# Row-wise cosine similarity: another order of rows for the loads, one square moved between engines, and the last load split

## Chip, cores, metric

The kernel runs on one core of one Trainium2 chip. Four of the core's engines occur here: ACT (ScalarE) and DVE (VectorE) compute, POOL (GpSimd) issues the loads, SP (SyncE) issues the store. The 16 DMA engines move the data in packets. The metric is the device time of one execution in microseconds, the median over several executions. A comparison is made between executions of two kernels on the same chip.

## The reference

```python
x = np.random.randn(8192, 8192).astype(np.float32)
y = np.random.randn(8192, 8192).astype(np.float32)

def reference(x, y):
    x_norm = np.linalg.norm(x, axis=1, keepdims=True)
    y_norm = np.linalg.norm(y, axis=1, keepdims=True)
    return np.sum(x * y, axis=1) / (x_norm.squeeze() * y_norm.squeeze() + 1e-8)
```

Two matrices of 268 MB each are read once. The output has 8192 numbers.

## The kernel before

Rows are spread over the 128 partitions (P = 128) as 64 tiles (T = 64) of 128 rows. Partition `p` of tile `t` holds row `64 p + t`, so within one load the rows of neighbouring partitions lie 64 rows, 2 MiB, apart. That distance is called the pitch here. The loads are issued from POOL and convert fp32 to fp16 on the way.

```python
    C1 = 5462 if C == 8192 else (2 * C) // 3
    x_re = x.rearrange("(p t) c -> t p c", t=T)
    y_re = y.rearrange("(p t) c -> t p c", t=T)
    out_re = out.rearrange("(p t) -> p t", t=T)
    data = ctx.enter_context(tc.tile_pool(name="data", bufs=2))
    # ... scratch and statistics tiles cut ...
    for t in range(T):
        x_tile = data.tile([P, C], fp16)
        y_tile = data.tile([P, C], fp16)
        nc.gpsimd.dma_start(out=x_tile, in_=x_re[t])
        nc.gpsimd.dma_start(out=y_tile, in_=y_re[t])
        # ACT: sum of x*x over the whole row; sum of y*y over the first C1 columns
        nc.scalar.activation(out=act_scr, in_=x_tile, func=Square, accum_out=nx2[:, t : t + 1])
        nc.scalar.activation(out=act_scr[:, :C1], in_=y_tile[:, :C1], func=Square,
                             accum_out=ny2a[:, t : t + 1])
        # DVE: sum of x*y over the whole row; sum of y*y over the other columns
        nc.vector.tensor_tensor_reduce(out=dve_scr, in0=x_tile, in1=y_tile, ...,
                                       accum_out=dot[:, t : t + 1])
        nc.vector.tensor_tensor_reduce(out=dve_scr[:, C1:], in0=y_tile[:, C1:],
                                       in1=y_tile[:, C1:], ..., accum_out=ny2b[:, t : t + 1])
    # ny2 = ny2a + ny2b; res = dot / (sqrt(nx2 * ny2) + 1e-8), all 128x64   (cut)
    nc.sync.dma_start(out=out_re, in_=res)
```

(`Square` stands for the long enum name; arguments are shortened.)

Of the kernel before, what the change touches and what calls it, by code (L numbers as in the profile page):

```python
# [1 line left out]

# [4 lines left out]


@with_exitstack
def kernel(  # L10
    ctx: ExitStack,
    tc: tile.TileContext,
    x: bass.AP,
    y: bass.AP,
    out: bass.AP,
):
    nc = tc.nc
    P = nc.NUM_PARTITIONS
    R, C = x.shape
    assert R % P == 0  # L20
    T = R // P

    fp32 = mybir.dt.float32
    fp16 = mybir.dt.float16

    C1 = 5462 if C == 8192 else (2 * C) // 3

    x_re = x.rearrange("(p t) c -> t p c", t=T)
    y_re = y.rearrange("(p t) c -> t p c", t=T)
    out_re = out.rearrange("(p t) -> p t", t=T)  # L30

    data = ctx.enter_context(tc.tile_pool(name="data", bufs=2))
    scratch = ctx.enter_context(tc.tile_pool(name="scratch", bufs=1))
    stats = ctx.enter_context(tc.tile_pool(name="stats", bufs=1))

    dve_scr = scratch.tile([P, C], fp16)
    act_scr = scratch.tile([P, C], fp16)

    nx2 = stats.tile([P, T], fp32)
    ny2a = stats.tile([P, T], fp32)  # L40
    ny2b = stats.tile([P, T], fp32)
    dot = stats.tile([P, T], fp32)
    res = stats.tile([P, T], fp32)

    for t in range(T):
        x_tile = data.tile([P, C], fp16)
        y_tile = data.tile([P, C], fp16)
        nc.gpsimd.dma_start(out=x_tile, in_=x_re[t])  # L48
        nc.gpsimd.dma_start(out=y_tile, in_=y_re[t])  # L49

        nc.scalar.activation(  # L51
            out=act_scr,
            in_=x_tile,
            func=mybir.ActivationFunctionType.Square,
            accum_out=nx2[:, t : t + 1],
        )
        nc.scalar.activation(  # L57
            out=act_scr[:, :C1],
            in_=y_tile[:, :C1],
            func=mybir.ActivationFunctionType.Square,  # L60
            accum_out=ny2a[:, t : t + 1],
        )
        nc.vector.tensor_tensor_reduce(  # L63
            out=dve_scr,
            in0=x_tile,
            in1=y_tile,
            scale=1.0,
            scalar=0.0,
            op0=mybir.AluOpType.mult,
            op1=mybir.AluOpType.add,  # L70
            accum_out=dot[:, t : t + 1],
        )
        nc.vector.tensor_tensor_reduce(  # L73
            out=dve_scr[:, C1:],
            in0=y_tile[:, C1:],
            in1=y_tile[:, C1:],
            scale=1.0,
            scalar=0.0,
            op0=mybir.AluOpType.mult,
            op1=mybir.AluOpType.add,  # L80
            accum_out=ny2b[:, t : t + 1],
        )

    ny2 = stats.tile([P, T], fp32)
    nc.vector.tensor_add(out=ny2, in0=ny2a, in1=ny2b)  # L85
    prod = stats.tile([P, T], fp32)
    nc.vector.tensor_mul(out=prod, in0=nx2, in1=ny2)  # L87
    denom = stats.tile([P, T], fp32)
    nc.scalar.activation(  # L89
        out=denom,  # L90
        in_=prod,
        func=mybir.ActivationFunctionType.Sqrt,
        bias=0.0,
        scale=1.0,
    )
    nc.vector.tensor_single_scalar(  # L96
        out=denom, in_=denom, scalar=1e-8, op=mybir.AluOpType.add
    )
    rden = stats.tile([P, T], fp32)
    nc.vector.reciprocal(out=rden, in_=denom)  # L100
    nc.vector.tensor_mul(out=res, in0=dot, in1=rden)  # L101

    nc.sync.dma_start(out=out_re, in_=res)


# [1 line left out]
_INS = ['x', 'y']  # L107
_OUTS = [((8192,), 'float32')]


# [23 lines left out]
```

## Time and profile before

| | before |
|---|---|
| median time | 1267.15 us |
| span of the profiled execution | 1265.6 us |
| first y tile ready for ACT | 25.5 us |
| last y tile ready for ACT | 1249.4 us |
| store of the result issued | 1263.2 us |

The page of the kernel before. "DMA" is the mean busy share of the 16 DMA engines in tenths, in 40 equal slices of the span. "GB/s" is what they wrote in each slice; the source bytes are twice that, because fp32 becomes fp16. The last line is the head of the chain of waits.

```profile
span 1265.6 us, 1011 instructions
DVE 751.0 (59%) x261; ACT 768.9 (61%) x259; POOL 67.9 (5%) x132
...
DMA  9999999999999999999999999999999999999994
GB/s 182 214 213 212 217 216 216 215 216 217 217 217 216 216 216 215 216 216 216 217 216 216 216 216 214 216 217 217 217 216 217 215 216 216 216 216 217 216 217 93
...
q0 software_dynamic: 18432, 268.44, 99.8%
...
DMA 96%; DVE 3%; issue 1%; POOL 0%; ACT 0%; DVEq 0%; POOLq 0%; PEldq 0%
```

The DMA engines never rest, and DVE and ACT do for 40% of the time. The kernel is bound by its loads. Stretches chosen by hand (columns: stretch in us, its length, busy time of DVE, ACT and POOL with instructions, clock, DMA share, GB/s written):

```profile
0.00:40.00 40.00, 11.71 (x4) 17.30 (x6) 3.51 (x10) 1.00 0.95 189
40.00:120.00 80.00, 46.85 (x16) 48.83 (x17) 4.22 (x8) 1.00 1.01 212
120.00:200.00 80.00, 46.85 (x16) 50.01 (x18) 4.22 (x8) 1.00 1.02 216
```

Part of the low first line is the start, before the first load runs.

Two lines from the start of the timeline of the kernel before, and its end (start, length, engine, line, operation, output<-inputs, and what ended the idle time before it). In the loop ACT waits for each load, so the starts of its squares tell when a load is ready. The first two lines are the second load, which is the first of y, and the eleventh:

```profile
25.47 4.75 ACT L57 ACTIVATE act_scr<-y_tile 128x5462 f16<-128x5462 f16 x1 [3.41 <-DMA y_tile<-in_y_dram]
...
115.01 7.03 ACT L51 ACTIVATE act_scr<-x_tile 128x8192 f16<-128x8192 f16 x1 [5.20 <-DMA x_tile<-in_x_dram]
...
1230.07 4.75 ACT L57 ACTIVATE act_scr<-y_tile 128x5462 f16<-128x5462 f16 x1 [2.51 <-DMA y_tile<-in_y_dram]
...
1249.44 4.75 ACT L57 ACTIVATE act_scr<-y_tile 128x5462 f16<-128x5462 f16 x1 [2.56 <-DMA y_tile<-in_y_dram]
1249.52 8.69 DVE L63 CUSTOM_DVE_ANT_0 dve_scr<-x_tile,y_tile 128x8192 f16<-128x8192 f16 x1 [7.63 <-DMA y_tile<-in_y_dram]
...
1258.25 3.00 DVE L73 CUSTOM_DVE_ANT_0 dve_scr<-y_tile 128x2730 f16<-128x2730 f16 x1
...
1262.99 0.23 DVE L101 TENSOR_TENSOR res<-dot,rden 128x64 f32<-128x64 f32 x1
1263.24 0.37 SPq L103 DMA_DIRECT2D out_dram<-res  x1
```

A y tile is ready every 19.37 us. After the last one nothing is left to load, and DVE's 8.69 and 3.00 us lie bare, then 2 us of small operations, then the store until 1265.6.

### The profile page before, as it was taken

The page shows a single profiled execution, that of the slowest core. Times are in us where ns is not written, and L with a number is a line of the kernel's source. Part 1 is how long each engine was busy: PE and PEld are TensorE (multiplying, and loading weights), DVE is VectorE, ACT ScalarE, POOL GpSimd, SP SyncE. Part 2 cuts the span into 40 slices and gives each one's busy share as a digit, 9 for nine tenths or more (in the row PEclk, how much of TensorE's full clock was granted, in tenths as well). Part 3 has the DMA queues.
Part 4 walks back from the last instruction along what each step waited for, and adds up shares of the span by engine and source line. Part 5 has one row for each costly group of instructions (what it writes and reads, how often), then busy time and mean ns, then how long its engine had stood idle before and what let it go on. Part 6 is the DMA issues. An engine that isn't in the chain of part 4 may idle for free.

```text
span 1265.6 us, 1011 instructions
## 1 busy us (share of the span) xinstructions
DVE 751.0 (59%) x261; ACT 768.9 (61%) x259; POOL 67.9 (5%) x132
## 2 busy tenths in 40 slices
DVE  1565655755656657557566565575565665755756
ACT  4656666666566566665665666656656656666564
POOL 0000000000000000000000000000000000000000
DMA  9999999999999999999999999999999999999994
GB/s 182 214 213 212 217 216 216 215 216 217 217 217 216 216 216 215 216 216 216 217 216 216 216 216 214 216 217 217 217 216 217 215 216 216 216 216 217 216 217 93
DMA packets 18584, 268.54 MB, mean 212 GB/s; under 512 B 2192, under 2 KB 2192, under 8 KB 2192
## 3 DMA queue, kind: packets, MB, share of 16 engines
q0 software_dynamic: 18432, 268.44, 99.8%
q14 instruction: 8, 0.07, 0.0%
q1 hardware_dynamic: 144, 0.03, 0.0%
HBM read 536.87 MB, written 0.03 MB: 424 GB/s over the span
## 4 chain that ended last, share of the span: by engine, by line
DMA 96%; DVE 3%; issue 1%; POOL 0%; ACT 0%; DVEq 0%; POOLq 0%; PEldq 0%
DMA y_tile<-in_y_dram 96%; DVE dve_scr L63 3%; DVE dve_scr L73 0%; POOL x_tile L48 0%; DVE rden L100 0%; POOL y_tile L49 0%; ACT denom L89 0%; DVE ny L85 0%; DVE prod L87 0%; DVE res L101 0%; DVE denom L96 0%; DVEq L63 0%; DVE dot L63 0%; DVEq L85 0%; POOLq L129 0%
## 5 line engine op out<-in xcount | busy, mean ns | idle before, releaser
L63 DVE CUSTOM_DVE_ANT_0 dve_scr<-x_tile,y_tile 128x8192 f16<-128x8192 f16 x64 | 556.3, 8693 | 509.5 <-DMA y_tile<-in_y_dram 509.5
L51 ACT ACTIVATE act_scr<-x_tile 128x8192 f16<-128x8192 f16 x64 | 449.9, 7030 | 321.9 <-DMA x_tile<-in_x_dram 321.9
L57 ACT ACTIVATE act_scr<-y_tile 128x5462 f16<-128x5462 f16 x64 | 304.3, 4755 | 164.3 <-DMA y_tile<-in_y_dram 164.3
L73 DVE CUSTOM_DVE_ANT_0 dve_scr<-y_tile 128x2730 f16<-128x2730 f16 x64 | 192.2, 3003 | 2.2
L48 POOL DMA_DIRECT2D x_tile<-in_x_dram x64 | 33.9, 530 | 996.8 <-DVE dot L63 996.0
L49 POOL DMA_DIRECT2D y_tile<-in_y_dram x64 | 33.8, 528 | 158.7 <-DVE ny2b L73 146.0
L57 ACT ACTIVATION_READ_ACCUMULATOR act_scr<-y_tile 128x1 f32 x64 | 11.9, 186 | 0.0
L51 ACT ACTIVATION_READ_ACCUMULATOR act_scr<-x_tile 128x1 f32 x64 | 11.9, 186 | 0.0
L73 DVE DVE_READ_ACCUMULATOR2_ANT ny2b<- 128x1 f32 x64 | 5.3, 83 | 0.0
L63 DVE DVE_READ_ACCUMULATOR2_ANT dot<- 128x1 f32 x64 | 5.3, 83 | 0.0
L89 ACT ACTIVATE denom<-prod 128x64 f32<-128x64 f32 x1 | 0.3, 256 | 6.3 <-DVE prod L87 6.3
L51 ACT ACT_TABLE_LOAD x1 | 1.3, 1283 | 0.7 <-PEq L118 0.7
L89 ACT ACT_TABLE_LOAD x1 | 1.3, 1283 | 0.0
L100 DVE RECIPROCAL rden<-denom 128x64 f32<-128x64 f32 x1 | 0.6, 553 | 0.0
L96 DVE TENSOR_SCALAR denom<-denom 128x64 f32<-128x64 f32 x1 | 0.2, 195 | 0.3 <-ACT denom L89 0.3
L85 DVE TENSOR_TENSOR ny<-ny2a,ny2b 128x64 f32<-128x64 f32 x1 | 0.2, 225 | 0.1
L101 DVE TENSOR_TENSOR res<-dot,rden 128x64 f32<-128x64 f32 x1 | 0.2, 226 | 0.0
L87 DVE TENSOR_TENSOR prod<-nx,ny 128x64 f32<-128x64 f32 x1 | 0.2, 224 | 0.0
L118 POOL MEMSET const-float32-0.0<- 128x1 f32 x1 | 0.1, 98 | 0.2 <-issue 0.2
L118 POOL MEMSET const-bfloat16-1.0<- 128x1 bf16 x1 | 0.1, 102 | 0.0
L118 POOL MEMSET const-float32-1.0<- 128x1 f32 x1 | 0.1, 98 | 0.0
L118 POOL MEMSET const-uint8-127<- 128x1 uint8 x1 | 0.1, 98 | 0.0
## 6 DMA issues: line engine op xcount, KB each, us to landing
x_tile<-in_x_dram POOLq DMA_DIRECT2D x64, 2048.0 KB, 19.7
y_tile<-in_y_dram POOLq DMA_DIRECT2D x64, 2048.0 KB, 26.3
out_dram<-res SPq DMA_DIRECT2D x1, 32.0 KB, 1.5
```

Source lines behind the costliest of these rows:

```text
L48: nc.gpsimd.dma_start(out=x_tile, in_=x_re[t])
L49: nc.gpsimd.dma_start(out=y_tile, in_=y_re[t])
L51: nc.scalar.activation(out=act_scr, in_=x_tile, func=mybir.ActivationFunctionType.Square, accum_out=nx2[:, t : t + 1],)
L57: nc.scalar.activation(out=act_scr[:, :C1], in_=y_tile[:, :C1], func=mybir.ActivationFunctionType.Square, accum_out=ny2a[:, t : t + 1],)
L63: nc.vector.tensor_tensor_reduce(out=dve_scr, in0=x_tile, in1=y_tile, scale=1.0, scalar=0.0, op0=mybir.AluOpType.mult, op1=mybir.AluOpType ...
L73: nc.vector.tensor_tensor_reduce(out=dve_scr[:, C1:], in0=y_tile[:, C1:], in1=y_tile[:, C1:], scale=1.0, scalar=0.0, op0=mybir.AluOpType.mult,
L85: nc.vector.tensor_add(out=ny2, in0=ny2a, in1=ny2b)
L87: nc.vector.tensor_mul(out=prod, in0=nx2, in1=ny2)
L89: nc.scalar.activation(out=denom, in_=prod, func=mybir.ActivationFunctionType.Sqrt, bias=0.0, scale=1.0,)
L96: nc.vector.tensor_single_scalar(out=denom, in_=denom, scalar=1e-8, op=mybir.AluOpType.add)
L100: nc.vector.reciprocal(out=rden, in_=denom)
L118: nc = _bacc.Bacc("TRN2", target_bir_lowering=False, num_devices=1)
```

## The change

There are three intents. The rows are grouped in blocks of 8, so that the pitch falls to 8 rows (256 KiB) and one load reads within 32 MiB instead of 256. The whole square of y goes to ACT. The last pair of tiles is loaded and worked through in pieces, so that less work is left after the last landing. The output is then stored in runs of 8 numbers (32 bytes) instead of 64.

```diff
-    C1 = 5462 if C == 8192 else (2 * C) // 3
-    x_re = x.rearrange("(p t) c -> t p c", t=T)      # y alike
-    out_re = out.rearrange("(p t) -> p t", t=T)
+    B = 8
+    x_re = x.rearrange("(a p b) c -> a b p c", p=P, b=B)      # y alike
+    out_re = out.rearrange("(a p b) -> p a b", p=P, b=B)
 ...
-    for t in range(T):
+    for t in range(T - 1):
-        nc.gpsimd.dma_start(out=x_tile, in_=x_re[t])
+        nc.gpsimd.dma_start(out=x_tile, in_=x_re[t // B, t % B])
 ...
         nc.scalar.activation(
-            out=act_scr[:, :C1], in_=y_tile[:, :C1],
+            out=act_scr, in_=y_tile,
 ...
-        nc.vector.tensor_tensor_reduce(     # DVE's part of y*y
-            out=dve_scr[:, C1:], in0=y_tile[:, C1:], in1=y_tile[:, C1:], ...
+    # last pair: x in 2 loads of 4096 columns, y in loads of 4096, 2048, 2048 columns;
+    # ACT squares each piece; DVE forms x*y over each piece of y
+    # five additions of 128x1 join the pieces; then prod, sqrt, + 1e-8, reciprocal, product
 ...
-    nc.sync.dma_start(out=out_re, in_=res)
+    nc.sync.dma_start(out=out_re, in_=res.rearrange("p (a b) -> p a b", b=B))
```

More of the change, by code (lines that the diff above doesn't have):

```diff
@@ L24 @@
     fp16 = mybir.dt.float16
-    C1 = 5462 if C == 8192 else (2 * C) // 3
-    x_re = x.rearrange("(p t) c -> t p c", t=T)
-    y_re = y.rearrange("(p t) c -> t p c", t=T)
-    out_re = out.rearrange("(p t) -> p t", t=T)
+    B = 8
+    x_re = x.rearrange("(a p b) c -> a b p c", p=P, b=B)
+    y_re = y.rearrange("(a p b) c -> a b p c", p=P, b=B)
+    out_re = out.rearrange("(a p b) -> p a b", p=P, b=B)
     data = ctx.enter_context(tc.tile_pool(name="data", bufs=2))
@@ L39, with finalize @@
     nx2 = stats.tile([P, T], fp32)
-    ny2a = stats.tile([P, T], fp32)
-    ny2b = stats.tile([P, T], fp32)
+    ny2 = stats.tile([P, T], fp32)
     dot = stats.tile([P, T], fp32)
     res = stats.tile([P, T], fp32)
-    for t in range(T):
+    prod = stats.tile([P, T], fp32)
+    denom = stats.tile([P, T], fp32)
+    rden = stats.tile([P, T], fp32)
+    def finalize(lo, hi):
+        s = slice(lo, hi)
+        nc.vector.tensor_mul(out=prod[:, s], in0=nx2[:, s], in1=ny2[:, s])
+        nc.scalar.activation(
+            out=denom[:, s],
+            in_=prod[:, s],
+            func=mybir.ActivationFunctionType.Sqrt,
+            bias=0.0,
+            scale=1.0,
+        )
+        nc.vector.tensor_single_scalar(
+            out=denom[:, s], in_=denom[:, s], scalar=1e-8, op=mybir.AluOpType.add
+        )
+        nc.vector.reciprocal(out=rden[:, s], in_=denom[:, s])
+        nc.vector.tensor_mul(out=res[:, s], in0=dot[:, s], in1=rden[:, s])
+    CH = C // 2
+    ycuts = [0, C // 2, (3 * C) // 4, C]
+    NYC = len(ycuts) - 1
+    nx2q = stats.tile([P, 2], fp32)
+    ny2q = stats.tile([P, NYC], fp32)
+    dotq = stats.tile([P, NYC], fp32)
+    H = T // 2
+    for t in range(T - 1):
         x_tile = data.tile([P, C], fp16)
         y_tile = data.tile([P, C], fp16)
-        nc.gpsimd.dma_start(out=x_tile, in_=x_re[t])
-        nc.gpsimd.dma_start(out=y_tile, in_=y_re[t])
+        nc.gpsimd.dma_start(out=x_tile, in_=x_re[t // B, t % B])
+        nc.gpsimd.dma_start(out=y_tile, in_=y_re[t // B, t % B])
         nc.scalar.activation(
@@ L57 @@
         nc.scalar.activation(
-            out=act_scr[:, :C1],
-            in_=y_tile[:, :C1],
+            out=act_scr,
+            in_=y_tile,
             func=mybir.ActivationFunctionType.Square,
-            accum_out=ny2a[:, t : t + 1],
+            accum_out=ny2[:, t : t + 1],
         )
@@ L72 @@
         )
+    tl = T - 1
+    x_tile = data.tile([P, C], fp16)
+    y_tile = data.tile([P, C], fp16)
+    for h in range(2):
+        cs = slice(h * CH, (h + 1) * CH)
+        nc.gpsimd.dma_start(out=x_tile[:, cs], in_=x_re[tl // B, tl % B][:, cs])
+    for j in range(NYC):
+        cs = slice(ycuts[j], ycuts[j + 1])
+        nc.gpsimd.dma_start(out=y_tile[:, cs], in_=y_re[tl // B, tl % B][:, cs])
+    for h in range(2):
+        cs = slice(h * CH, (h + 1) * CH)
+        nc.scalar.activation(
+            out=act_scr[:, cs],
+            in_=x_tile[:, cs],
+            func=mybir.ActivationFunctionType.Square,
+            accum_out=nx2q[:, h : h + 1],
+        )
+    for j in range(NYC):
+        cs = slice(ycuts[j], ycuts[j + 1])
+        nc.scalar.activation(
+            out=act_scr[:, cs],
+            in_=y_tile[:, cs],
+            func=mybir.ActivationFunctionType.Square,
+            accum_out=ny2q[:, j : j + 1],
+        )
         nc.vector.tensor_tensor_reduce(
-            out=dve_scr[:, C1:],
-            in0=y_tile[:, C1:],
-            in1=y_tile[:, C1:],
+            out=dve_scr[:, cs],
+            in0=x_tile[:, cs],
+            in1=y_tile[:, cs],
             scale=1.0,
@@ L80 @@
             op1=mybir.AluOpType.add,
-            accum_out=ny2b[:, t : t + 1],
+            accum_out=dotq[:, j : j + 1],
         )
-    ny2 = stats.tile([P, T], fp32)
-    nc.vector.tensor_add(out=ny2, in0=ny2a, in1=ny2b)
-    prod = stats.tile([P, T], fp32)
-    nc.vector.tensor_mul(out=prod, in0=nx2, in1=ny2)
-    denom = stats.tile([P, T], fp32)
-    nc.scalar.activation(
-        out=denom,
-        in_=prod,
-        func=mybir.ActivationFunctionType.Sqrt,
-        bias=0.0,
-        scale=1.0,
-    )
-    nc.vector.tensor_single_scalar(
-        out=denom, in_=denom, scalar=1e-8, op=mybir.AluOpType.add
-    )
-    rden = stats.tile([P, T], fp32)
-    nc.vector.reciprocal(out=rden, in_=denom)
-    nc.vector.tensor_mul(out=res, in0=dot, in1=rden)
-    nc.sync.dma_start(out=out_re, in_=res)
+    nc.vector.tensor_add(out=nx2[:, tl : tl + 1], in0=nx2q[:, 0:1], in1=nx2q[:, 1:2])
+    nc.vector.tensor_add(out=ny2q[:, 0:1], in0=ny2q[:, 0:1], in1=ny2q[:, 1:2])
+    nc.vector.tensor_add(out=ny2[:, tl : tl + 1], in0=ny2q[:, 0:1], in1=ny2q[:, 2:3])
+    nc.vector.tensor_add(out=dotq[:, 0:1], in0=dotq[:, 0:1], in1=dotq[:, 1:2])
+    nc.vector.tensor_add(out=dot[:, tl : tl + 1], in0=dotq[:, 0:1], in1=dotq[:, 2:3])
+    finalize(0, T)
+    nc.sync.dma_start(out=out_re, in_=res.rearrange("p (a b) -> p a b", b=B))
 _INS = ['x', 'y']
```

## The prediction

> **What bounds the kernel.** Reading. The slices show the DMA engines at 90% or more in 39 of 40 slices; the software queue holds 99.8% of 16 engines' span. DVE is 59% busy, ACT 61%. The chain of waits is 95.5% y loads; POOL waits 996 us for the dot product to free x buffers, but in time: at 1220.0 us it issues an x load, while the DMA still has 10 us of y queued ahead of it. In steady state a pair of tiles lands every 19.37 us (y landings at 1210.7, 1230.0, 1249.4): 8.39 MB of fp32 read in that time is 433 GB/s. The Trainium skill ("DMA: Bandwidth & Descriptors", Where 436 GB/s comes from) puts the fabric's limit at 435 GB/s; the trace agrees to 0.5% if the source bytes are counted. So the loop can hardly get faster.
>
> **Tail now.** The last y lands at 1249.4. Then come the dot product (8.69 us), DVE's share of the y square (3.00), about 2.0 of small operations, and the output store from 1263.2 to 1265.6 (2.4).
>
> **What the change does.**
> 1. DVE's y share (192 us in all) moves to ACT: per pair DVE falls from 11.7 to 8.8 us, ACT rises from 12.1 to about 14.4 (7.03+0.19, twice), still under 19.37. Worth nothing in 63 of 64 pairs; y loads are issued about 2.5 us sooner, into a queue that is already full.
> 2. Row layout: the pitch between partitions falls from 2 MiB to 256 KiB. The same Trainium skill page (Latency and other measured facts) reports copies losing rate at 2 MiB pitch, 164 against 214 GB/s. This trace does not show that loss: 433 GB/s is read at 2 MiB. The layout should thus give nothing, perhaps 1 to 3 us of the early slices that run at 212 to 214 GB/s instead of 217.
> 3. Split last tile. The slope between DVE's two shapes (8.69 us for 8192, 3.00 for 2730) gives 1.04 ns an element plus 0.16 us, hence 4.43, 2.29, 2.29 us for the y pieces of 4096, 2048, 2048. The first piece lands about 4.8 us before the last. DVE then works through a backlog and ends about 4.6 us after the last landing, where before it needed 11.9. ACT ends at about +2.9, its table load (1.28) at +4.2: hidden. Five additions of 128x1, estimated at 0.19 each, cost +0.95; one 128x64 addition goes (-0.25). The result is ready at about +7.2 instead of +13.86: 6.6 us saved.
> 4. Output: pieces of 32 bytes instead of 256, about 1024 data packets instead of 128, so 64 per engine instead of 8. The 256-byte packets took 18 ns each; an estimate is +1 to +2 us at the very end, all exposed.
> 5. Three more loads, smaller packets: +0.1 to 0.3 us.
>
> Sum: 1267.15 - 6.6 + 1.3 + 0.2 = about **1262 us** (-0.4%). Range 1256.5 to 1266. Chances: faster by over 2% 0.02, within 2% 0.95, slower 0.03.
>
> **What would show it.** The steady pair period stays at 19.3 to 19.5 us, mean rate 216 GB/s written; DVE busy falls by about 190 us and ACT rises by about 145 with the time hardly moving; the last DVE dot piece ends 4 to 5 us after the last y landing; the store takes 3.3 to 4.5 us from issue to the end; ACT's table load isn't on the chain.
>
> **What would make it wrong.** HBM answers differently to the 256 KiB pitch (slices well off 216 all along); the 32-byte store costs over 3 us and eats the tail's gain; the last pieces land unevenly across engines, so that the small ones come together and the backlog grows; 128x1 additions cost much more than estimated.

## More of the kernel before

The experiments ran on four chips, called chip 7, 9, 1 and 10 after the number in their records. The number of the chip of the first pair of runs isn't recorded.

## The result, and the profile after

The changed kernel takes **1255.94 us** (median of 7 executions, 1255.76 to 1256.43), the kernel before 1267.15 us. The ratio is 0.991, with a 95% interval of 0.990 to 0.992. The gain of 11.2 us is twice the predicted 5.1, and the time lies just below the range given.

From the page of the changed kernel:

```profile
span 1254.2 us, 902 instructions
DVE 558.7 (45%) x141; ACT 915.0 (73%) x265; POOL 69.5 (6%) x135
...
GB/s 198 216 214 216 217 217 218 217 216 216 216 215 217 218 217 217 217 216 216 217 216 215 217 217 217 217 217 216 216 217 214 217 217 217 217 217 217 216 216 139
```

Its stretches:

```profile
0.00:40.00 40.00, 8.70 (x2) 22.36 (x6) 3.53 (x10) 1.00 0.96 202
40.00:120.00 80.00, 34.80 (x8) 57.27 (x18) 4.25 (x8) 1.00 1.02 217
120.00:200.00 80.00, 36.80 (x9) 59.06 (x17) 4.21 (x8) 1.00 1.02 216
```

And the same two loads and the end of its timeline:

```profile
23.49 7.03 ACT L82 ACTIVATE act_scr<-y_tile 128x8192 f16<-128x8192 f16 x1 [2.59 <-DMA y_tile<-in_y_dram]
...
110.66 7.03 ACT L76 ACTIVATE act_scr<-x_tile 128x8192 f16<-128x8192 f16 x1 [2.56 <-DMA x_tile<-in_x_dram]
...
1225.17 7.03 ACT L82 ACTIVATE act_scr<-y_tile 128x8192 f16<-128x8192 f16 x1 [2.56 <-DMA y_tile<-in_y_dram]
...
1239.92 4.42 DVE L124 CUSTOM_DVE_ANT_0 dve_scr<-x_tile,y_tile 128x4096 f16<-128x4096 f16 x1 [5.97 <-issue]
...
1246.48 2.29 DVE L124 CUSTOM_DVE_ANT_0 dve_scr<-x_tile,y_tile 128x2048 f16<-128x2048 f16 x1
...
1247.39 1.28 ACT L49 ACT_TABLE_LOAD   x1
1248.69 0.09 DVE L124 DVE_READ_ACCUMULATOR2_ANT dotq<- 128x1 f32 x1
...
1250.85 0.22 DVE L60 TENSOR_TENSOR res<-dot,rden 128x64 f32<-128x64 f32 x1
1251.10 0.41 SPq L140 DMA_DIRECT2D out_dram<-res  x1
```

The y tile of the last pair but one is ready at 1225.2 instead of 1230.1, so 4.9 us were won before the tail begins. Early on, the stretch from 40 to 120 us now runs at the full rate, and the eleventh load is ready at 110.7 instead of 115.0 (starts of ACT's squares in the two timelines): 4.35 of the 4.9 us come from the first eleven loads.

The last landing isn't a wait in this timeline, because DVE and ACT are behind by then. By the completion events in the traces the last load landed at 1244.7 us, and at 1249.4 in the kernel before (the last data packets end 0.3 us earlier in both). The spans then divide like this:

| part | before | after | difference | predicted |
|---|---|---|---|---|
| until the last landing | 1249.4 | 1244.7 | -4.7 | +0.2 |
| last landing to issue of the store | 13.9 | 6.4 | -7.5 | -6.6 |
| store to the end | 2.3 | 3.1 | +0.7 | +1.3 |
| span | 1265.6 | 1254.2 | -11.4 | -5.1 |

### The profile page after: what moved, and what is told of

The parts are those of the page before. It is cut to its first block, busy times and chain, and to the rows that moved or that the text cites. A ratio compares the mean times of both kernels' runs of the same rounds, so it can differ in the third digit from the quotient of the medians. Undisturbed runs are those within 1.5% of the kernel's fastest.

```text
span 1254.2 us, 902 instructions
## 1 busy us (share of the span) xinstructions
DVE 558.7 (45%) x141; ACT 915.0 (73%) x265; POOL 69.5 (6%) x135
## 4 chain that ended last, share of the span: by engine, by line
DMA 93%; issue 5%; ACT 1%; DVE 1%; POOL 0%; POOLq 0%; DVEq 0%; PEldq 0%; ACTq 0%
DMA y_tile<-in_y_dram 93%; ACT act_scr L82 1%; DVE dve_scr L124 0%; POOL x_tile L73 0%; POOL x_tile L104 0%; DVE rden L59 0%; POOL y_tile L74 0%; ACT denom L49 0%; DVE prod L48 0%; DVE res L60 0%; DVE denom L56 0%; DVE ny L136 0%; DVE dot L138 0%; DVE dotq L124 0%; DVE dotq L137 0%
## 5 line engine op out<-in xcount | busy, mean ns | idle before, releaser
L88 DVE CUSTOM_DVE_ANT_0 dve_scr<-x_tile,y_tile 128x8192 f16<-128x8192 f16 x63 | 547.6, 8693 | 685.8 <-DMA y_tile<-in_y_dram 685.8
L76 ACT ACTIVATE act_scr<-x_tile 128x8192 f16<-128x8192 f16 x63 | 442.8, 7029 | 171.6 <-DMA x_tile<-in_x_dram 171.6
L82 ACT ACTIVATE act_scr<-y_tile 128x8192 f16<-128x8192 f16 x63 | 442.9, 7030 | 161.2 <-DMA y_tile<-in_y_dram 161.2
L124 DVE CUSTOM_DVE_ANT_0 dve_scr<-x_tile,y_tile 128x2048 f16<-128x2048 f16 (+1 forms) x3 | 8.8, 3000 | 6.0 <-issue 6.0
L118 ACT ACTIVATE act_scr<-y_tile 128x2048 f16<-128x2048 f16 (+1 forms) x3 | 7.4, 2468 | 0.2 <-DMA y_tile<-in_y_dram 0.2
L110 ACT ACTIVATE act_scr<-x_tile 128x4096 f16<-128x4096 f16 x2 | 7.2, 3608 | 0.0
L76 ACT ACT_TABLE_LOAD x1 | 1.3, 1283 | 0.7 <-PEq L155 0.7
L49 ACT ACT_TABLE_LOAD x1 | 1.3, 1283 | 0.0
```

The costliest lines, as they stand in the source:

```text
L49: nc.scalar.activation(out=denom[:, s], in_=prod[:, s], func=mybir.ActivationFunctionType.Sqrt, bias=0.0, scale=1.0,)
L76: nc.scalar.activation(out=act_scr, in_=x_tile, func=mybir.ActivationFunctionType.Square, accum_out=nx2[:, t : t + 1],)
L82: nc.scalar.activation(out=act_scr, in_=y_tile, func=mybir.ActivationFunctionType.Square, accum_out=ny2[:, t : t + 1],)
L110: nc.scalar.activation(out=act_scr[:, cs], in_=x_tile[:, cs], func=mybir.ActivationFunctionType.Square, accum_out=nx2q[:, h : h + 1],)
L118: nc.scalar.activation(out=act_scr[:, cs], in_=y_tile[:, cs], func=mybir.ActivationFunctionType.Square, accum_out=ny2q[:, j : j + 1],)
L124: nc.vector.tensor_tensor_reduce(out=dve_scr[:, cs], in0=x_tile[:, cs], in1=y_tile[:, cs], scale=1.0, scalar=0.0, op0=mybir.AluOpType.mult ...
```

## Experiments

Theory A: the first reads at a pitch of 2 MiB are slow, and the new layout takes that away. (A place, below, is the stretch of memory from which one partition reads its rows. At a pitch of 2 MiB there are 128 of x and 128 of y.) Rival B: because DVE no longer squares y, its tiles come free sooner, y loads are issued 2.5 us earlier, and a fuller queue gives the loop its gain. B is weakened already by the trace: the first four loads are issued before any tile comes free, and they are where 3.2 us of the 4.35 arise.

### e1: the row layout alone

```diff
-    x_re = x.rearrange("(p t) c -> t p c", t=T)      # y alike
-    out_re = out.rearrange("(p t) -> p t", t=T)
+    B = 8
+    x_re = x.rearrange("(a p b) c -> a b p c", p=P, b=B)      # y alike
+    out_re = out.rearrange("(a p b) -> p a b", p=P, b=B)
```

(with the indexing and the store that go with it; nothing else of the kernel before is touched)

> Only the row layout (pitch 256 KiB, output in pieces of 32 bytes) in the kernel before. Theory A (the 2 MiB pitch makes the first reads slow): the first y tile is ready near 23.5 us instead of 25.5, the eleventh load is ahead by 4.3 us, the store costs 0.75 us more: about 1263.2 us. Rival B (y loads issued earlier, because DVE no longer squares y, fill the queue): nothing gained in the loop, the store costs 0.75: about 1267.9 us.

Measured: 1263.19 us (1263.06 to 1263.69), correct. The time of theory A is met, and so are its early loads: the first y tile is ready at 23.44 us, the eleventh load at 110.60. But the kernel before took **1293.87 us** on this chip (chip 7; 1286.55 to 1302.97 in 11 executions), so the ratio is 0.976. The layout alone is worth 31 us here.

### e2: the changed kernel with the layout undone

```diff
-    x_re = x.rearrange("(a p b) c -> a b p c", p=P, b=B)      # y alike
-    out_re = out.rearrange("(a p b) -> p a b", p=P, b=B)
+    x_re = x.rearrange("(p t) c -> t p c", t=T)      # y alike
+    out_re = out.rearrange("(p t) -> p t", t=T)
```

> The changed kernel with the row layout undone (pitch 2 MiB, output in pieces of 256 bytes). Theory A: the slow first reads are back (+4.7 us), the store is 0.75 us shorter: about 1259.9 us. Rival B: the loop keeps its gain and the store gets shorter: about 1255.2 us.

Measured on chip 7: 1291.26 us (1290.23 to 1292.67), correct; ratio to before 0.997 (0.994 to 1.001). Both times expected are missed, since neither knew of this chip. The direction is A's: without the layout the loop's gain is gone. The row of GB/s by slice of this run shows where:

```profile
GB/s 173 207 210 215 216 213 213 213 214 214 210 213 213 209 208 213 208 209 214 204 212 210 211 211 207 216 214 215 214 215 209 213 215 212 214 211 213 213 210 115
```

On this chip a 2 MiB pitch is slow throughout, though not evenly (most slices lie between 204 and 216). In the packet records 2243 of its 16 KB packets took over 1.24 us, where the usual one takes 1.227; these are called slow below. The kernel before on its own chip had 318 of them, 201 in the first 120 us. In e1, on the same chip as e2, there were 21. What slow packets took beyond 1.227 us, summed and divided by the 16 DMA engines, is called their excess: 28.6 us in e2, 4.5 in the kernel before, of which 3.5 fall in the first 120 us.

### e3: the square of y on ACT, alone

```diff
-            out=act_scr[:, :C1],
-            in_=y_tile[:, :C1],
+            out=act_scr,
+            in_=y_tile,
 ...
-        nc.vector.tensor_tensor_reduce(     # DVE's part of y*y, and the addition of the parts
-            out=dve_scr[:, C1:], ...
```

> The kernel before with the whole square of y on ACT, nothing else. Theory A: only the tail gains, DVE's 3.00 us of y square and one addition of 0.25: about 1263.9 us; the first loads as slow as before (first y near 25.5 us, ACT starting on it). Rival B: 4 to 5 us more are gained in the loop: about 1259.2 us.

Measured on chip 7: 1292.76 us (1287.87 to 1297.43), correct; ratio 0.999 (0.995 to 1.003). Inconclusive in size, as 3 us drown in this chip's scatter. No sign of a gain in the loop, against B. It was run again as e11.

### e4: the pitch switched in the middle

```diff
-        nc.gpsimd.dma_start(out=x_tile, in_=x_re[t])
+        nc.gpsimd.dma_start(out=x_tile, in_=x_lo[t // 8, t % 8] if t < 32 else x_re[t])      # y alike
```

`x_lo` is the layout with blocks of 8 rows, over rows 0 to 4095. The result is wrong.

> Wrong result on purpose: in the kernel before, tiles 0 to 31 read rows 0 to 4095 at a pitch of 256 KiB, tiles 32 to 63 read as before at 2 MiB, so that half of the 2 MiB regions are read for the first time near 625 us. Theory A1 (a first read of many far apart places at once is slow): the first loads are as fast as in the changed kernel (-4.4 us by the eleventh load), and 1 to 4.4 us are lost again within some six loads after 625 us: 1264 to 1267 us. Theory A2 (a 2 MiB pitch is slow only at the start, while the DMA engines run in step): nothing is lost near 625 us, about 1262.8 us.

Measured on chip 7: 1281.38 us (1278.74 to 1284.56). Both times are missed, for the chip is slow at 2 MiB in any case. The first half had one slow packet after the first load, and the others began at the switch (623.5 us). To tell more, a chip was wanted on which the slow packets end by themselves. That came with e13.

### e5: as far apart, but no power of two

```diff
-        nc.gpsimd.dma_start(out=x_tile, in_=x_re[t])      # row 64 p + t
+        nc.gpsimd.dma_start(out=x_tile, in_=x_63[t])      # row 63 p + t; y alike
```

The result is wrong: partition p reads row 63 p + t.

> Wrong result on purpose: the kernel before, with partition p of tile t reading row 63 p + t instead of 64 p + t, so that the pitch is 2 MiB less 32 KiB: as far apart as before, but no power of two. Theory P (the power of two makes the reads collide): no slow packets, neither early (first y ready near 23.5 us) nor later, about 1262.4 us on any chip (the layout-only run less 0.75 us for its store). Theory F (first reads of many far apart places are slow): the early loads are as slow as in the kernel before (first y ready at 25.4 us or later), and 3 to 5 us of the loss stay. On a chip on which the kernel before takes 1294 us the two may share the loss: P takes away the slow packets from 200 us on, F keeps those of the first 120 us.

Measured on chip 9, where the kernel before takes 1267.27 us: 1262.65 us (1262.52 to 1262.68); ratio 0.996 (0.995 to 0.997). The first y tile is ready at 23.6 us, 20 packets are slow instead of hundreds, and the rate from 40 to 120 us is 216 GB/s (columns as above):

```profile
40.00:120.00 80.00, 46.84 (x16) 48.32 (x18) 4.22 (x8) 1.00 1.01 216
```

Theory F, in the form that a first read of far apart places is slow whatever the pitch, falls. The power of two matters, as theory P has it: places nearly as far apart, at a pitch of 2016 KiB, are read at the full rate from the start. (This is one other pitch; no more were tried.)

### e6 and e9: short reads ahead of the loads

```diff
+    first = scratch.tile([P, 2, 4, 64], fp16)
+    for k, src in enumerate((x, y)):
+        nc.gpsimd.dma_start(
+            out=first[:, k],
+            in_=src.rearrange("(p t) c -> p t c", t=T)[:, 0:4, 0:64],
+        )
     for t in range(T):
```

In e6 this stands in the kernel before. In e9 it stands in the kernel of e5, with t=63 in place of T.

> The kernel before, with two short loads ahead of all others that read 256 bytes of the rows that tiles 0 to 3 begin with, from each of the 128 places of x and of y. They delay the first load by 1 to 3 us. Theory F: the slow part moves into these short loads, which wait for all places at once; the four following loads then take 9.7 us each, and by the eleventh load the kernel is 1 to 3 us ahead of the kernel before. Theory P: the loads behind them are as slow as before, and the whole is 1 to 3 us behind the kernel before.

> Wrong result on purpose: the run with a pitch of 63 rows plus the same two short loads ahead, from its own 128 places of x and of y. If the short loads took their 10 us (first load ready at 25.3 us instead of 14.9) because the places lie a power of two apart, they take clearly less here: first load ready near 16 to 19 us, total about 1265 to 1268 us. If short casting loads take that long anyway, the first load is ready near 24 to 25 us again and the total is about 1273 us; then the run with the short loads ahead says less about the places.

Measured: e6 1274.93 us (1274.25 to 1275.54) on chip 9, correct, 7.7 us over the kernel before there (ratio 1.006). e9 1264.16 us (1264.10 to 1264.78) on chip 1, only 1.5 us over e5's 1262.65, and 0.8 below the range expected; its first load is ready at 15.3 us, also a little earlier than expected. The issue lines of the two traces (output<-source, queue, operation, count, KB written, us from issue to landing), e6 first:

```profile
first<-in_x_dram POOLq DMA_DIRECT2D x1, 64.0 KB, 8.7
first<-in_y_dram POOLq DMA_DIRECT2D x1, 64.0 KB, 13.1
```

```profile
first<-in_x_dram POOLq DMA_DIRECT2D x1, 64.0 KB, 2.7
first<-in_y_dram POOLq DMA_DIRECT2D x1, 64.0 KB, 3.0
```

The same number of equally short reads takes 3.2 and 4.4 times as long when the rows lie 2 MiB apart. So short reads that convert aren't slow by themselves. And after them, in e6, the large loads at 2 MiB pitch run at nearly the full pace: ready at 25.3, 35.1, 45.0 and 54.7 us, where the kernel before had 14.9, 25.5, 36.0 and 46.0. The slow part moved into the short reads, and got dearer there: the total expected (1 to 3 us behind) was missed by 5 us. The four loads came close to the 9.7 us each of theory F (9.6 to 9.9 from one to the next), but the eleventh load is ready 8 us behind the kernel before, not ahead. P and F each explain a part: whole rows are read slowly where the pitch is a power of two, and mainly for the first time. It is the full pace of the loads behind the short reads that speaks for the first time, not the slowness of the short reads. e13 and e14 test that.

### e7: 1 MiB

```diff
-    B = 8
+    B = 32
```

(of e1)

> The layout-only kernel with blocks of 32 rows: pitch 1 MiB, output in pieces of 128 bytes. Both P and F expect something between the kernel before and the layout-only run: on a chip on which the kernel before takes 1267 us, 1263 to 1266 us; on one on which it takes 1294 us, 1265 to 1285 us. A time within 1 us of the layout-only run (1263.2) would say that the effect is gone already at 1 MiB.

Measured on chip 9: 1265.80 us (1264.64 to 1266.73), correct; ratio 0.998 (0.997 to 1.000). 138 packets were slow. As expected, the time lies between the two. With 1265.80 against e5's 1262.65 on the same chip, where the kernel before has 1267.27, some two thirds of the loss stay at half the pitch.

### e13 and e14: first reads, or going over to this pitch

e13 is e4 again. e14 reads at 2 MiB first, then at 256 KiB, then at 2 MiB again:

```diff
-        nc.gpsimd.dma_start(out=x_tile, in_=x_re[t])
+        nc.gpsimd.dma_start(out=x_tile, in_=x_re[t] if t < 8 else x_lo[t // 8 - 1, t % 8] if t < 32 else x_re[t - 24])
```

(y alike; wrong results)

> Wrong result on purpose, the switch in the middle again, for a chip on which the kernel before takes about 1267 us. Theory F2 (at a power-of-two pitch, reads of places not read before are slow): tiles 64 to 67 of the loads (near 625 us) show 1 to 2.5 us of slow packets together, and near 0 after load 76; total about 1263.5 to 1265 us. Theory S (only the start of the program is slow, with the engines in step): none at the switch; about 1262.5 us.

> Wrong result on purpose: tiles 0 to 7 at 2 MiB, 8 to 31 at 256 KiB, then on at 2 MiB with the rows that follow those of tile 7. Slow packets at loads 0 to 10 as in the kernel before. F2: none at the switch back (loads 64 to 67 together under 0.3 us), since rows beside those now read were read at the start. If going over to the power-of-two pitch is slow by itself, with or without earlier reads: 1 to 2.5 us there as in the run with one switch.

Measured on chip 10, where the kernel before takes 1268.29 us: e13 1266.99 us (1266.35 to 1267.80), e14 1267.54 us (1266.63 to 1268.09). The stretch behind the switch in e13, and the same in e14 (columns as above):

```profile
620.00:700.00 80.00, 46.85 (x16) 47.52 (x17) 4.24 (x8) 1.00 1.01 210
```

```profile
620.00:700.00 80.00, 47.56 (x18) 50.40 (x17) 4.77 (x9) 1.00 1.01 216
```

ACT's start on the last load before the switch and on the sixteenth behind it, in e13 and in e14:

```profile
624.23 4.75 ACT L60 ACTIVATE act_scr<-y_tile 128x5462 f16<-128x5462 f16 x1 [2.62 <-DMA y_tile<-in_y_dram]
...
783.28 4.75 ACT L60 ACTIVATE act_scr<-y_tile 128x5462 f16<-128x5462 f16 x1 [2.58 <-DMA y_tile<-in_y_dram]
```

```profile
628.27 4.75 ACT L60 ACTIVATE act_scr<-y_tile 128x5462 f16<-128x5462 f16 x1 [2.56 <-DMA y_tile<-in_y_dram]
...
783.34 4.75 ACT L60 ACTIVATE act_scr<-y_tile 128x5462 f16<-128x5462 f16 x1 [2.58 <-DMA y_tile<-in_y_dram]
```

In e13 the sixteen loads from the switch on take 159.05 us, in e14 155.07 (differences of these starts). So a loss of nearly the size of the start's, 4.0 us, appears in the middle of the program when half of the places are read for the first time at this pitch, and doesn't appear when rows beside them have been read before. Why half of the places cost nearly the whole loss, these runs don't show. In the packet records, loads 64 to 67 (counted from 0) hold 1.1 us of excess in e13 (expected 1 to 2.5) and none in e14; e14's early loads hold 3.2 us, much as in the kernel before. e13's total lies 2 us above the expected, as the loss went on over sixteen loads and not four. Theory S, that only the start of the program is slow, falls. So does the thought that going over to this pitch costs something by itself.

### e10 and e11: the parts again, with e12, the whole, on the same chip

The edits are those of e2 and e3; e12 is the changed kernel.

> The changed kernel with the row layout undone, again, for a chip on which the kernel before takes about 1267 us. There: tail as in the changed kernel (7.4 us less than before), the early loss of 4.3 us back, a store 0.75 us shorter: about 1259.9 us, 0.994 of the kernel before. On a chip on which the kernel before takes over 1285 us, 2 to 9 us below it, as in the first such run.

> The kernel before with the whole square of y on ACT, again. On a chip on which the kernel before takes about 1267 us: 3.25 us less in the tail and nothing in the loop, about 1263.9 us; a rival that puts the loop's gain on the earlier issue of the y loads says 1259 to 1260.

> The changed kernel itself on the same chip as its parts: about 1256 us on any chip[...]; near 0.991 of the kernel before where that takes 1267 us, near 0.971 where that takes 1294 us.

All three ran on chip 1, were correct, and were compared with 1267.67 us for the kernel before:

| kernel | median us | ratio to before (95%) |
|---|---|---|
| e11: y's square on ACT | 1264.28 | 0.998 (0.996 to 0.999) |
| e10: that, and the last pair split | 1261.64 | 0.995 (0.994 to 0.996) |
| e12: that, and the layout | 1255.92 | 0.991 (0.990 to 0.992) |

e11 is A's 1263.9 within its scatter (1263.22 to 1266.49), and not B's 1259 to 1260. B falls. e12 is as expected. e10 was expected at 1259.9 and lies 1.7 us above it. Its timeline shows one reason:

```profile
1230.91 7.03 ACT L81 ACTIVATE act_scr<-y_tile 128x8192 f16<-128x8192 f16 x1 [2.53 <-DMA y_tile<-in_y_dram]
...
1249.79 1.91 ACT L117 ACTIVATE act_scr<-y_tile 128x2048 f16<-128x2048 f16 x1 [0.23 <-DMA y_tile<-in_y_dram]
...
1252.85 1.91 ACT L117 ACTIVATE act_scr<-y_tile 128x2048 f16<-128x2048 f16 x1 [1.06 <-DMA y_tile<-in_y_dram]
```

From the y tile of the last pair but one to the last piece it takes 21.9 us; with the layout, 19.5. ACT now waits for the last piece instead of being behind it. So the split loads are slower at 2 MiB (e2 shows 25.8 us for the same on chip 7), and the layout is worth something in the tail as well. The packet records show that the packets themselves are slower: of the 256 packets of 4 KB (the y pieces of 2048 columns) 171 took longer than the 324 ns that all of them take in e12, 468 ns in the mean. Over the 16 engines this makes 2.3 us, and the 8 KB packets add 0.2: the whole difference. These are no first reads of their places, since 63 tiles have been read from beside them. So a 2 MiB pitch costs time beyond first reads as well, here where each row is read in shorter pieces. Why was not tried.

### e8: a shorter tail

```diff
-    ycuts = [0, C // 2, (3 * C) // 4, C]
+    cuts = [0, C // 2, (3 * C) // 4, (7 * C) // 8, C]      # x and y pieces loaded in turn
 ...
+    # one Sqrt at the very start, so that its table serves the squares too
+    # columns 0 to 55 are finished and stored after tile 56; DVE squares the last piece of x
```

> The changed kernel with a shorter tail: last pair loaded in four pieces of x and y in turn (4096, 2048, 1024, 1024 columns), so that DVE has no backlog when the last lands; one sqrt table from the start; 56 of 64 output columns stored early. The last landing stays near 1244.6 to 1245.2 us; DVE's last piece ends about 1.5 us after it instead of 4.2; the result is ready at +3 us instead of +6.5; the store takes 2.3 instead of 3.1: about 1251.8 us, 4 less than the changed kernel's 1255.94.

Measured on chip 9: 1252.49 us (1252.33 to 1253.10), correct; ratio 0.988 (0.987 to 0.989) to the kernel before, 3.4 us below the changed kernel's median on chip 1. The two were not run on one chip, but the changed kernel's median was 1255.94 and 1255.92 in both calls that ran it. It is the fastest version, 0.7 us short of what was expected. Its last load landed at 1245.5 us, 0.8 later than the changed kernel's. This was lost early: its eleventh load is ready at 111.40 us instead of 110.66, with 299 slow packets between 12 and 120 us that hold 0.7 us of excess. At a pitch of 256 KiB no other run here shows so many; why is not known. The end of its timeline:

```profile
1247.78 0.16 DVE L131 TENSOR_REDUCE ny<-nyq 128x1 f32<-128x4 f32 x1 [0.81 <-ACT act_scr L123]
...
1249.06 0.35 SPq L136 DMA_DIRECT2D out_dram<-res  x1
```

DVE has no backlog any more, but now ACT has: it comes late from the last full tile, and DVE waits 0.81 us for its last square.

## Why the prediction was wrong

- **What bounds the kernel** was right: loads in the loop, a bare tail after them. DVE's busy time fell by 192 us and ACT's rose by 146 (predicted 190 and 145), and none of that was to be seen in the loop, as e11 shows.
- **The layout was the step that failed.** The prediction said: "The layout should thus give nothing, perhaps 1 to 3 us of the early slices that run at 212 to 214 GB/s instead of 217", and put 0 into its sum. It gave 4.7 us until the last landing, 4.35 of them in the first eleven loads; on one chip, e12 is 5.7 us faster than e10, which differs from it in the layout alone. The step went wrong where it took the steady rate at the end of the trace, 433 GB/s, as proof that a 2 MiB pitch costs nothing. The early slices showed the cost, and the prediction had read them, but didn't count it. The Trainium skill ("DMA: Bandwidth & Descriptors", Latency and other measured facts) reports a loss at large powers of two, for copies between two tensors in memory; on this kernel's loads it shows mainly in reads of places not read before (e13 against e14), it goes with the power of two and not with the distance (e5, and e6 against e9), on one of the chips it doesn't end (e2), and it returns where rows are read in shorter pieces (e10).
- **The tail was right in kind and mis-sized**: 7.5 us saved instead of 6.6. DVE ended 4.1 us after the last landing instead of the 4.6 given: its three pieces took 8.85 us together (1239.92 to 1248.77), not quite the sum of 9.01 that the prediction worked out, and the first piece landed 4.9 us before the last. The five additions took 0.8 us (1248.69 to 1249.48), not 0.95.
- **The store** costs 0.7 us more, not 1.3: a 32-byte packet took 7 ns, a 256-byte one 18.
- **ACT's table load** was hidden, as predicted: it ends at 1248.7, the product that the square root waits for at 1249.7.
- Together: -4.7 instead of +0.2, -7.5 instead of -6.6, +0.7 instead of +1.3. The first of these terms is 4.9 us of the 6.3 missed in the span, and the layout is behind it.

What stays open: how the reads come to be slow; no run here looks into it. It is open as well why chip 7 stays slow at 2 MiB for the whole program (27 us above the other chips for the same kernel, at the same granted clock), whether a pitch of 63 rows would help there (256 KiB does), and why the packets of split loads are slower at 2 MiB.

## What to carry to other kernels

When all rates but those of the first few per cent of the span are at their peak, ask what is special about the first accesses, and count the loss in the prediction. Rows that one load takes from memory at a pitch of a large power of two are worth moving closer together, even where a trace from one chip shows little loss: another chip may pay more for the same loads (31 us on chip 7). After the loop, cut the last load so that what remains after its landing is small on every engine, and look at all of them, as the backlog moves from one engine to the next.

## What the Trainium skill lacked or had wrong

- "DMA: Bandwidth & Descriptors", Latency and other measured facts, row on HBM row pitch: it gives 164 instead of 214 GB/s for a pitch of 2 MiB, independent of how many tiles are touched, for copies between two tensors in memory on other queues. These are loads that convert, issued from POOL. At 2 MiB they read 430 to 433 GB/s of source bytes in the steady state on chips 9, 1 and 10 (215 to 216 GB/s written from 1120 to 1200 us in e6, e10, e11, e13 and e14); the loss is 4 to 5 us, most of it in first reads. On chip 7 it lasts, and costs 27 us of 1294. That chips differ is not on the page, nor that first reads are slower than later ones. That a small step away from the power of two helps is on it (+4 KiB), and e5 agrees with -32 KiB.
- The same page, Where 436 GB/s comes from: it puts the limit of 435 GB/s on the ports of the on-chip memory. These loads halve their bytes on the way and write only 216 GB/s there, and still stop at 433 GB/s of source bytes. So the figure fits here only if the source bytes are counted; which part of the path sets it, no run here tells.
- "ScalarE: Activation LUTs", What ACT_TABLE_LOAD costs: it gives 1283 ns for a table load, which the traces show to the digit, and 1380 ns of draining, 2.66 us in all for a switch. The draining didn't show here: in e10 1.31 us passed from the end of ACT's last square (1254.86, with its read-out) to the start of the square root (1256.17). That a Sqrt issued first leaves a table which serves the squares too isn't on the page: with Square first there were two loads, in e8 one.
- No page gives the cost of a store in 32-byte runs to memory: 1024 runs instead of 128 of 256 bytes took 0.7 us more, at 7 ns a packet instead of 18.
